# Layer 1's feed-forward as block products, modulation rows dealt out anew, and the chain on block-diagonal 128x128 weights

## The chip, the cores and the metric

One core of a Trainium2 chip runs the whole program. The metric is device microseconds for one execution, the median of the runs; each kernel is also profiled once. The engines are named PE (matrix products; its weight loads are shown apart as PEld), DVE (vector), ACT (scalar functions), POOL (GpSimd) and SP (issues the DMA transfers). Each engine works through its own queue in order and waits for others through semaphores.

## The reference

A two-layer transformer step over 128 prompt tokens and 512 sample tokens, which the kernel treats as T = 640 columns, in two halves of HF = 320. All values are fp32. For each layer:

```python
mod = silu(cond) @ w_mod[l] + b_mod[l]              # 6 x 1024 values for each of 2 conditions
sh_a, sc_a, g_a, sh_f, sc_f, g_f = split(mod, 6)
xn = rmsnorm(h, norm_mix) * (1 + sc_a) + sh_a
proj = xn @ w_in[l]
# three branches (attention, gated linear attention, gated delta net), gates, output projection
h = h + g_a * y
xf = rmsnorm(h, norm_ffn) * (1 + sc_f) + sh_f
gu = xf @ ffn_w_in[l]                               # 1024 -> 2 x 2816
h = h + g_f * ((silu(gu[..., :D_FF]) * gu[..., D_FF:]) @ ffn_w_out[l])
```

The delta net walks over chunks of 64 tokens, 8 heads, in both directions:

```python
v_new = u_n - w_n @ s
o_n   = qd_n @ s + a_n @ v_new
s     = ge_n * s + ke_n.T @ v_new
```

## The kernel before

**The weight stream.** Most of PE's work is one long list of jobs, held by the object `G` (class `Stream`): every 128-column tile of every weight matrix, in a fixed order. A unit of a job takes 4 blocks of 128 rows. Its weights come by DMA into `wr`, are split on ACT (`wh`, the rounded high part, line 514) and on POOL or DVE (`wl`, the rest, lines 518 and 516), and each block makes three products, high x high, high x low, low x high, each on 320 columns, into the PSUM tile `gm`. So one output tile on 8 blocks is 48 matmuls 128x320. When a job ends, its `post` is called (evacuation). `G.to(name)` runs the stream to the end of a job; `fill(name)` slips in as much of the stream as the table `FILL` says at this place. `ahead()` issues the loads for some two units ahead and the split of the next one. Instructions are placed into each engine's queue by a planner which takes the earliest in program order that its model holds ready; an instruction wrapped in `o(...)` while `strict[0]` is set, or given to `keep_in_program_order`, keeps its place.

**Feed-forward.** Output tiles fg (gate) and fu (up) come in 22 pairs. A plain pair is 96 matmuls. The second layer (l = 1 in the code) makes only the first 3 pairs plain (`NPL`), the other 19 as block products: the 2x2 blocks (gate/up x first/second half of the rows) times (row halves x token halves) with 7 block products (`PRODS`) in place of 8, each of 12 matmuls (line 555), so 84 a pair. DVE makes the four sums of weight blocks (`ws`), the low halves `wl` of all seven, and the sums of results (class `Blocks`); ACT takes snapshots of PSUM (`snap`). These are in program order. The 22 tiles are in groups (`GROUPS`): after each group the output products fo (8 of them, over the group's 7, 8 or 11 blocks) are added to h (`h_update`, line 756). The first layer (l = 0) makes all 22 pairs plain, in two groups of 11.

**Modulation.** 16 of the 48 rows of the first layer's `mod` are made on PE at the start. The others, and all of the second layer's, are made on DVE by `ModVe.steps`: a row of weights (`wmt`) by DMA, then two products with sum (line 638), one for each condition. With `nh` = 2 a row comes in two halves of 512 (two tiles, four products), with `nh` = 1 in one of 1024 (two products). Before: rows 16 to 35 of the first layer in its chain (`nh` = 2, one product at each site, the rest after the loop), 36 to 39 in wo, 40 to 47 and all 48 of the second layer in the posts of fu of the first layer's feed-forward (`nh` = 1, kept in program order). The buffers for `wmt` are 4.

**The chain.** `gdn_chain` walks over the delta net's chunks for one pair of heads p; four pairs a layer, on the two directions at once, with 10 steps. A step has up to three products for each direction: with k (result `cy`, line 1066), with t (results `vs` on DVE, line 1078, and `VN` on ACT, line 1081), with kt (new state `S`, line 1092), with `fill` between them and a modulation site (`msite` 3) after the last. `mm_heads` makes each product as two matmuls, one for each head, on 64x64 weights that lie on the partitions of the head (line 1041). After the loop come the products with q (line 1115, block-diagonal 128x128 already) and a, the norm, and five transposes. `chain_load` brings t0, t1, k, kt, q, a of the next pair.

## Time and profile before

| | us |
|---|---|
| median of 3 runs | 2867.09 (2866.7 to 2870.57) |
| profiled execution | 2866.79 |
| its span (first to last instruction) | 2865.0 |
| PE busy | 2681.8 (94%) |
| DVE, ACT, POOL busy | 1699.1, 1290.1, 1075.7 |
| first layer: chain, then wo, then feed-forward | about 644 to 893, to 972, to 1457 |
| second layer: chain, then merge and wo, then feed-forward | about 2075 to 2314, to 2394, to 2853 |

The stages are read off the timeline by the lines that only they use. A row of the timeline merges neighbouring instructions of one kind: start, length, engine, line, operation, tiles (out<-in), shapes (weights rows\*columns, then moving), count, and in brackets the idle time before it with what ended it. The length of a matmul holds its run through the pipeline, so the pace is read from the starts.

### The profile page before, as it was taken

To read this page: it belongs to the slowest core of one execution; us is meant where nothing else is said; L and a number is where in the kernel's file an instruction comes from. 1 tells how busy PE (TensorE), PEld (TensorE's weight loads), DVE (VectorE), ACT (ScalarE), POOL (GpSimd) and SP (SyncE) were. 2 spreads that over 40 slices of the span, in tenths; PEclk is the share of its full clock that TensorE was granted. 3 is DMA by queue.
4 is the path that set the end of the run, shared out by engine and by line. 5 is a ranking of instruction groups with operands and counts; after the bars stand their busy time and mean duration, and the time that the engine had idled before them with its cause. 6 is when DMAs were issued, how large, how long until landed. Compare 5 with 4: busy or idle time off the path is not lost. (4 is left out here: it accounts for less than half of the span.)

```text
span 2865.0 us, 49715 instructions
## 1 busy us (share of the span) xinstructions
PE 2681.8 (94%) x19216; PEld 2461.6 (86%) x19216; DVE 1699.1 (59%) x3141; ACT 1290.1 (45%) x2431; POOL 1075.7 (38%) x777
## 2 busy tenths in 40 slices
PE   6889999899999999999998899997999998999998
PEld 4788887787878899999988888886877898999997
DVE  4765684647655699268456666757434345637373
ACT  5665655543333522122356646565333336425254
POOL 3543222343425467456544432333433254120203
PEclk9999999999999999999999999998999999999999
DMA  6254433245542355335323444232433331222222
GB/s 207 90 163 142 94 77 100 81 113 175 151 113 86 133 175 181 107 123 159 114 80 106 152 136 95 73 97 76 118 98 84 84 108 52 85 85 78 78 80 79
DMA packets 291836, 317.10 MB, mean 111 GB/s; under 512 B 163696, under 2 KB 174768, under 8 KB 291472
## 3 DMA queue, kind: packets, MB, share of 16 engines
q1 hardware_dynamic: 291600, 313.92, 37.4%
q8 instruction: 152, 2.49, 0.4%
q14 instruction: 84, 0.69, 0.1%
HBM read 266.01 MB, written 47.82 MB: 110 GB/s over the span
## 5 line engine op out<-in xcount | busy, mean ns | idle before, releaser
L518 POOL TENSOR_TENSOR wl<-wr,wh 128x512 fp32r<-128x512 f32 (+1 forms) x500 | 723.3, 1450 | 1407.0 <-ACT wh L514 1287.0
L563 PE MATMUL gm<-xh,wh 128*128 128x320 f32 x2848 | 706.2, 324 | 25.6 <-ACT xh L713 7.0
L563 PE MATMUL gm<-xl,wh 128*128 128x320 f32 x2848 | 692.0, 318 | 10.1 <-DVE xl L720 4.2
L563 PE MATMUL gm<-xh,wl 128*128 128x320 f32 x2848 | 687.3, 317 | 15.0 <-POOL wl L518 15.0
L514 ACT ACTIVATE wh<-wr 128x512 fp32r<-128x512 f32 (+1 forms) x538 | 332.4, 621 | 703.7 <-PE gm L563 441.6
L563 PEld LDWEIGHTS gm<-xh,wh 128*128 128x128 f32 x2848 | 487.3, 193 | 50.9 <-ACT xh L713 9.9
L563 PEld LDWEIGHTS gm<-xl,wh 128*128 128x128 f32 x2848 | 491.8, 192 | 27.0 <-DVE xl L720 9.0
L563 PEld LDWEIGHTS gm<-xh,wl 128*128 128x128 f32 x2848 | 489.5, 192 | 23.9 <-POOL wl L518 17.5
L638 DVE CUSTOM_DVE_ANT_0 ctb<-wmt,cbb 128x1024 f32<-128x1024 f32 (+1 forms) x200 | 298.2, 1491 | 3.4
L756 DVE SCALAR_TENSOR_TENSOR h<-gm,mod,h 128x128 f32<-128x128 f32 x168 | 63.8, 433 | 248.7 <-PE gm L563 248.6
L563 PE MATMUL gm<-ah,wh 128*128 128x320 f32 x704 | 164.2, 310 | 0.4 <-DVE h L756 0.2
L563 PE MATMUL gm<-ah,wl 128*128 128x320 f32 x704 | 163.3, 309 | 0.5 <-POOL wl L518 0.5
L563 PE MATMUL gm<-al,wh 128*128 128x320 f32 x704 | 163.3, 309 | 0.0
L1081 ACT ACTIVATE VN<-ch 64x64 f32<-64x64 f32 x320 | 69.9, 219 | 179.7 <-DVE vs L1078 165.5
L563 PEld LDWEIGHTS gm<-ah,wh 128*128 128x128 f32 x704 | 118.3, 188 | 1.7 <-DVE h L756 1.4
L563 PEld LDWEIGHTS gm<-ah,wl 128*128 128x128 f32 x704 | 118.4, 188 | 0.8 <-POOL wl L518 0.8
L563 PEld LDWEIGHTS gm<-al,wh 128*128 128x128 f32 x704 | 118.5, 188 | 0.2
L563 PE MATMUL gm<-ol,wh 128*128 128x320 f32 x384 | 99.0, 331 | 1.5 <-POOL ol L568 1.5
L563 PE MATMUL gm<-oh,wh 128*128 128x320 f32 x384 | 98.4, 333 | 0.5 <-DVE gth L1756 0.3
L563 PE MATMUL gm<-oh,wl 128*128 128x320 f32 x384 | 96.1, 326 | 0.0
L555 PE MATMUL gm<-xh,wl 128*128 128x320 f32 x304 | 94.0, 309 | 0.0
L555 PE MATMUL gm<-xl,wh 128*128 128x320 f32 x304 | 93.9, 309 | 0.0
(793 smaller groups left out, 4743.8 us busy)
## 6 DMA issues: line engine op xcount, KB each, us to landing
wr<-in_wall_dram SPq DMA_DIRECT2D x394, 256.0 KB, 3.0
wmt<-in_wmodt_dram SPq DMA_DIRECT2D x60, 512.0 KB, 3.7
wr<-in_wfo_dram SPq DMA_DIRECT2D x64, 256.0 KB, 2.7
wr<-in_wbr_dram SPq DMA_DIRECT2D x48, 256.0 KB, 2.7
wmt<-in_wmodt_dram SPq DMA_DIRECT2D x40, 256.0 KB, 3.4
wq<-in_wall_dram SPq DMA_DIRECT2D x38, 256.0 KB, 3.1
wm<-in_wmod_dram SPq DMA_DIRECT2D x16, 512.0 KB, 8.4
wr<-in_wfo_dram SPq DMA_DIRECT2D x32, 192.0 KB, 2.4
```

Of the source, the lines that this page charges most:

```text
L514: o(se.activation(wh[:, :w], wr[:, :w], AF.Copy))
L518: ge.tensor_tensor(wl[:, :w], wr[:, :w], wh[:, :w], op=ALU.subtract)
L555: o(pe.matmul(ps, w_[:, wsl], x_[k], start=(start and i == 0), stop=(stop and i == 2), skip_group_check=True))
L563: o(pe.matmul(ps[:, c, :HF], w_[:, wsl], x_[kx][:, c * HF:(c + 1) * HF], start=(start and i == 0), stop=(stop and i == 2)))
L638: ins = ve.tensor_tensor_reduce(self.t, wm, self.c[:, i], 0.5, 0.0, ALU.mult, ALU.add, accum_out=acc[h][:, m - m0, i:i + 1])
L756: o(ve.scalar_tensor_tensor(hs[d][:, s:e], ps[:, c, s - c * HF:e - c * HF], g[:, d, i:i + 1], hs[d][:, s:e], op0=ALU.mult, op1=ALU.add))
L1081: se.activation(VN[d * 64:(d + 1) * 64, h, n], ps[h * 64:(h + 1) * 64, 1], AF.Copy)
```

## The change

The first layer's feed-forward takes the second's form (3 plain pairs, 19 as block products, groups of 8, 7, 7). Its fu posts no longer make all modulation: rows 40 to 47 are begun in wo and ended in the posts of fu1 and fu2; of the second layer's 48 rows the first 24 are made behind the posts of fo (five products, four, four), rows 24 to 39 in the second layer's chain, 40 to 47 in its wo. All use `nh` = 2 with two buffers. Each modulation site of the chain makes two products. t0, t1, k and kt lie block-diagonally in 128x128, with zeros set once by memsets; `mm_heads` becomes one matmul. The tiles o, t and o2 of the chain move to the shared ring `th`, and the ring of snapshots has three slots in place of four. The gate function of the first layer's feed-forward becomes Silu, as in the second, and the factor 0.5 of its row group 5 goes.

```diff
-GROUPS = (((0, 11), (11, 22)), ((0, 8), (8, 15), (15, 22)))
-NPL = (22, 3)
+GROUPS = ((0, 8), (8, 15), (15, 22))
+NPL = 3
...
-                        if OPT["pin"] in (1, 2 + self.nh):
+                        if strict[0] or OPT["pin"] in (1, 2 + self.nh):
...
-        elif s == 2 or s == 5 and mod is mods[0]:
+        elif s == 2:
...
-            if n in ("k", "kt"):
-                dma(B[n], SPL[n][p])
-                continue
...
-                elif n == "q":
+                elif n in ("q", "k", "kt"):
                     dma(B[n][hh, :, hh], SPL[n][p, hh])
                 else:
-                    dma(B[n][hh], TB[int(n[1])][p, h].rearrange("n s c -> s n c"))
-
-    def mm_heads(out, w, x):
-        for h in range(2):
-            hh = slice(h * 64, (h + 1) * 64)
-            pe.matmul(out[hh], w[hh], x[hh], start=True, stop=True)
+                    dma(B[n][hh, :, hh], TB[int(n[1])][p, h].rearrange("n s c -> s n c"))
...
-                    mm_heads(ps[:, 0], B["k"][:, n], S[:, n, d])
+                    pe.matmul(ps[:, 0], B["k"][:, n], S[:, n, d], start=True, stop=True)
...
-                mm_heads(ps[:, 1], B[f"t{d}"][:, n], y)
+                pe.matmul(ps[:, 1], B[f"t{d}"][:, n], y, start=True, stop=True)
...
-                    mm_heads(ps[:, 2], B["kt"][:, n], vs)
+                    pe.matmul(ps[:, 2], B["kt"][:, n], vs, start=True, stop=True)
...
-        o = kp.tile([P, NCH, 64], F32, name="co", tag="co")
-        t = kp.tile([P, 2, 5, 64], F32, name="ct", tag="ct")
+        o = vn(tmp())
+        t = tmp().rearrange("p (d j v) -> p d j v", d=2, j=5)
...
-        o2 = kp.tile([P, NCH, 64], F32, name="co2", tag="ct")
+        o2 = vn(tmp())
...
-            t = self.s[q.name, i] = self.sn.tile([P, HF], F32, name="sn", tag="sn", bufs=4)
+            t = self.s[q.name, i] = self.sn.tile([P, HF], F32, name="sn", tag="sn", bufs=3)
...
-                    for n in ("t0", "t1", "k", "kt"):
-                        bufs[n] = bd.tile([P, NCH, 64], F32, name="bd_" + n)
-                    bufs["q"] = bd.tile([P, NCH, P], F32, name="bd_q")
-                    mst = ModVe(bd, 4, 2).steps(0, range(16, 16 + OPT["mc"])) if l == 0 else iter(())
-                    for h in range(2):
-                        ge.memset(bufs["q"][h * 64:(h + 1) * 64, :, (1 - h) * 64:(2 - h) * 64], 0.0)
+                    for n in ("t0", "t1", "kt", "k", "q"):
+                        bufs[n] = bd.tile([P, NCH, P], F32, name="bd_" + n)
+                    mst = ModVe(bd, 2, 2).steps(l, range(16, 16 + OPT["mc"]) if l == 0 else range(24, 40))
+                    for n in ("t0", "t1", "kt", "k", "q"):
+                        for h in range(2):
+                            ge.memset(bufs[n][h * 64:(h + 1) * 64, :, (1 - h) * 64:(2 - h) * 64], 0.0)
                     chain_load(0, bufs, ("t0", "t1", "k", "kt"))
                     chain_load(0, bufs, ("q", "a"))
...
-                        gdn_chain(l, p, SC, bufs, kp, z[p], fill, lambda: next(mst, None))
+                        gdn_chain(l, p, SC, bufs, kp, z[p], fill, lambda: (next(mst, None), next(mst, None)))
...
-                    if l == 0:
-                        mod_fix(mod, prm, 2)
+                    for s_ in (2,) if l == 0 else (3, 4):
+                        mod_fix(mod, prm, s_)
...
-        mv = ModVe(mvp, 4, 1) if l + 1 < L else None
+        mv = ModVe(mvp, 2, 2)
+
+        def some(gen, n):
+            for _ in range(n):
+                if next(gen, 0) == 0:
+                    break
+
+        mv0 = mv.steps(l, range(16 + OPT["mc"], 40)) if l == 0 else iter(())
+        mv1 = mv.steps(l, range(40, 48))
+        nxt = mv.steps(l + 1, range(24)) if l + 1 < L else iter(())
         nm = Norm()
         resid_posts([f"wo{d}.{l}" for d in range(8)], hs, mod[:, 16:24], nm)
         for d in range(7):
             G.to(f"wo{d}.{l}")
-            if l == 0:
-                mv.run(0, range(16 + OPT["mc"] + (24 - OPT["mc"]) * min(d, 5) // 5, 16 + OPT["mc"] + (24 - OPT["mc"]) * min(d + 1, 5) // 5))
+            if l == 0 and d < 4:
+                some(mv0, 4)
+            else:
+                some(mv1, 5)
+        some(mv0, 1000)
         if l == 0:
             mod_fix(mod, prm, 3)
             mod_fix(mod, prm, 4)
+        else:
+            some(mv1, 1000)
+            mod_fix(mod, prm, 5)
...
-                    if l == 0:
-                        se.activation(v3(th), ps, AF.Tanh, scale=0.5)
-                        ve.scalar_tensor_tensor(v3(th), v3(th), 1.0, ps, op0=ALU.add, op1=ALU.mult)
-                    else:
-                        se.activation(v3(th), ps, AF.Silu)
+                    se.activation(v3(th), ps, AF.Silu)
...
-                    if l + 1 < L:
-                        if l == 0 and f < 8:
-                            mv.run(0, [40 + f])
-                            if f == 7:
-                                mod_fix(mod, prm, 5)
-                        mv.run(l + 1, range(48 * f // NF, 48 * (f + 1) // NF))
+                    if l == 0 and f:
+                        some(mv1, 8 if f < npl - 1 else 1000)
+                        if f == npl - 1:
+                            mod_fix(mod, prm, 5)
...
+            def fo_post(gi, d):
+                def post(ps):
+                    h_update(hs, d, ps, mod[:, 40:48])
+                    some(nxt, 4 if gi else 5)
+                return post
...
-                        G.posts[f"fo{gi}_{d}.{l}"] = lambda ps, d=d: h_update(hs, d, ps, mod[:, 40:48])
+                        G.posts[f"fo{gi}_{d}.{l}"] = fo_post(gi, d)
             nm = Norm()
             resid_posts([f"fo{gl_}_{d}.{l}" for d in range(8)], hs, mod[:, 40:48], nm, l + 1 < L)
+            for d in range(6):
+                n = f"fo{gl_}_{d}.{l}"
+
+                def after(*args, post=G.posts[n]):
+                    post(*args)
+                    some(nxt, 4)
+                G.posts[n] = after
...
-                for s_ in range(6):
+                some(nxt, 1000)
+                for s_ in range(3):
                     mod_fix(mods[l + 1], prms[l + 1], s_)
```

## Rows read from the trace of the kernel before

**Rows 1.** Windows: busy us (instructions) of PE, PEld, DVE, ACT, POOL; granted clock; DMA share, GB/s.

```profile
644.00:893.00 249.00, 243.03 (x2061) 196.28 (x2060) 156.98 (x475) 85.78 (x237) 79.16 (x64) 0.98 0.45 130
2075.00:2314.00 239.00, 233.79 (x2036) 189.93 (x2036) 93.44 (x307) 82.67 (x232) 73.08 (x63) 0.99 0.32 86
972.00:1457.00 485.00, 477.84 (x3198) 472.67 (x3197) 316.09 (x392) 128.74 (x217) 273.19 (x167) 0.99 0.43 133
2394.00:2853.00 459.00, 448.17 (x2981) 441.29 (x2979) 259.54 (x465) 210.57 (x366) 89.41 (x68) 0.99 0.24 73
```

**Rows 2.** Window of 55 us inside the second layer's block products.

```profile
2465.00:2520.00 55.00, 55.00 (x377) 55.00 (x376) 42.05 (x73) 29.75 (x54) 0.00 (x0) 1.00 0.26 82
```

**Rows 3.** Timeline of PE around two bursts of the chain.

```profile
666.20 0.31 PE L563 MATMUL gm<-xh,wh 128*128 128x320 f32 x1
666.44 0.33 PE L1041 MATMUL ch<-vs,bd_kt 64*64 64x64 f32 x4
666.71 0.41 PE L563 MATMUL gm<-xh,wh 128*128 128x320 f32 x1
666.95 0.45 PE L563 MATMUL gm<-xl,wh 128*128 128x320 f32 x2
...
2292.00 0.45 PE L563 MATMUL gm<-xh,wl 128*128 128x320 f32 x2
2292.39 0.45 PE L1041 MATMUL ch<-S,bd_k 64*64 64x64 f32 x8
2292.77 0.56 PE L563 MATMUL gm<-xh,wh 128*128 128x320 f32 x2
2293.16 0.45 PE L563 MATMUL gm<-xl,wh 128*128 128x320 f32 x2
```

**Rows 4.** Timeline of PE: the first and the last of 332 bursts.

```profile
645.51 0.45 PE L1041 MATMUL ch<-cvt,bd_t 64*64 64x64 f32 x8 [0.82 <-DMA cvt<-spl_vt]
...
2298.91 0.28 PE L1041 MATMUL ch<-cy__23305,bd_t 64*64 64x64 f32 x4
```

**Rows 5.** Timeline of PE: small products on 128*128 weights.

```profile
44.58 0.95 PE L608 MATMUL pmt<-C_base,mr 128*128 128x2 f32 x8
...
1577.72 1.05 PE L923 MATMUL pk<-kq,kbd 128*128 128x128 f32 x8
1578.53 0.54 PE L563 MATMUL gm<-xh,wh 128*128 128x320 f32 x2
1578.90 0.45 PE L563 MATMUL gm<-xl,wh 128*128 128x320 f32 x2
```

**Rows 6.** Timeline: one step of the second layer's chain.

```profile
2150.41 0.45 PE L1041 MATMUL ch<-S,bd_k 64*64 64x64 f32 x8
...
2152.14 0.92 ACT L1081 ACTIVATE VN<-ch 64x64 f32<-64x64 f32 x4
...
2153.35 0.33 PE L1041 MATMUL ch<-vs,bd_kt 64*64 64x64 f32 x4
...
2154.39 0.39 PE L1041 MATMUL ch<-S,bd_k 64*64 64x64 f32 x6
```

**Rows 7.** Groups of instructions by line and shape: busy us, mean ns.

```profile
L638 DVE CUSTOM_DVE_ANT_0 ctb<-wmt,cbb 128x512 f32<-128x512 f32 x80 | 68.7, 859 | 0.3
```

**Rows 8.** Timeline: from fo to blocks, second layer.

```profile
2580.34 1.13 DVE L756 SCALAR_TENSOR_TENSOR h<-gm,mod,h 128x128 f32<-128x128 f32 x3 [5.31 <-PE gm L563]
...
2581.39 1.28 DVE L516 TENSOR_TENSOR wl<-ws,wh 128x512 fp32r<-128x512 f32 x2
...
2582.19 0.35 PE L555 MATMUL gm<-xh,wl 128*128 128x320 f32 x1
```

**Rows 9.** Timeline of DVE: one product that runs alone.

```profile
690.76 0.68 DVE L638 CUSTOM_DVE_ANT_0 ctb<-wmt,cbb 128x512 f32<-128x512 f32 x1
```

**Rows 10.** DMA issues by line: count, KB each, median us to landing.

```profile
wmt<-in_wmodt_dram SPq DMA_DIRECT2D x40, 256.0 KB, 3.4
```

**Rows 11.** Waits of the SP queue, first layer's feed-forward: total us, times, longest.

```profile
SPq L429 <- DVE mod L638: 162.7, 50, 4.5
```

More of the change, by code (lines that the diff above doesn't have):

```diff
@@ L1678, in tile_hybrid @@
             k8(f"wo{d}", "post" if d == 7 else None)
-        gr, npl = GROUPS[l], NPL[l]
+        gr, npl = GROUPS, NPL
         pairs = {f: Pair(f"ff{f}.{l}", a["wall"][l, TILES[f"fg{f}"]], a["wall"][l, TILES[f"fu{f}"]]) for f in range(npl, NF)}
@@ L1981, in tile_hybrid @@
             mod_fix(mod, prm, 4)
+        else:
+            some(mv1, 1000)
+            mod_fix(mod, prm, 5)
         mark(f"normf{l}")
-        gr, npl = GROUPS[l], NPL[l]
+        gr, npl = GROUPS, NPL
         if npl < NF:
```

## The prediction

> **What bounds the kernel now.** I read the stretches by stage first [rows 1]: in both chain stages and both feed-forwards PE is busy 97 to 99% of the time, at a granted clock of 0.98 to 0.99 (the upper level, 2.4 GHz); apart from PE's own weight loads nothing passes 66%. So time is saved by giving PE less to do, unless something else becomes late where PE was the cover. "Busy" hides one thing, though, and the reader should look at starts rather than durations. In an undisturbed stretch PE starts 377 matmuls in 55.00 us, 0.146 us each [rows 2]; I use 0.147. Against that grid the timeline around the chain's small matmuls shows holes [rows 3].
>
> **The chain: what a burst costs.** From the start of the pair of gm matmuls at 2292.00 to the start of that at 2293.16 pass 1.16 us; the two pairs take 0.59 of it, so the burst of 8 passes on 64\*64 weights costs 0.57 [rows 3]. From 666.20 to 666.95 pass 0.75 us with two gm matmuls (0.29): a burst of 4 costs 0.46. Four more passes add 0.11 to 0.12, about 0.03 each; the rest, 0.34, is a constant for each burst, before it and after it. Counting uninterrupted bursts over both layers gives 332 [rows 4]. The passes are 56 calls a pair (18 with k, 20 with t, 18 with kt) x 2 heads x 2 passes (a call on fp32 shows as 2 instructions a head) x 8 pairs = 1792. Price now: 332 x 0.34 + 1792 x 0.03 = 113 + 54 = 167 us.
>
> After, each call is one matmul on 128\*128 weights: 896 passes of 64 columns. No row has that shape, so it is bounded by 128 columns and by 2. Eight passes on 128\*128 with 128 columns start at 1577.72, with no idle time noted before them; then follow a pair of gm at 1578.53 and the next pair at 1578.90. Less the first pair's 0.29, 1.18 leaves 0.89 for eight, 0.111 each. With 2 columns, eight passes last 0.95 against 1.05 [rows 5]: a difference of 0.10 over all eight, no more than the last one's own length, so the pace hardly depends on the columns and 64 of them should cost the same 0.111. New price 896 x 0.111 = 100 us, without a constant. PE's relief is 167 - 100 = 67 us.
>
> The Trainium skill, TensorE: Matmul & The Clock Gate, Part 3 (packing small matmuls by row and column tiling), speaks against this: tiles on different row groups run side by side, so two small matmuls cost hardly more than one. By that rule alone a pair of heads is already cheap, the block-diagonal form is a loss of 100 - 54 = 46 us, and the sum below would end at +37 us. The rows agree on the 0.03 us a pass and disagree on the 0.34 around each burst, which the rule leaves out.
>
> **How much of the relief arrives.** The chain is also a sequence of waits, and with shorter bursts these come to the front. A step of the second layer [rows 6]: k at 2150.41, VN (four copies, 0.92 us) from 2152.14, so until 2153.06, the second kt at 2153.35, the next k at 2154.39: 3.98 us. Without gm in between, the second kt can follow VN's end at once (0.28 earlier). The next k starts 1.04 after kt; a 0.28 us update of S and some 0.5 us of passing on between the engines are needed, so about 0.2 can go. Together 0.45 to 0.5 off, a floor near 3.5 us. In 80 steps that is 36 us: the lower bound, if the waits set the pace everywhere; 67 is the upper, if PE does. The stretches between the pairs of heads are full of gm and give what PE gives. I take 50.
>
> Against it stand the modulation rows. The second layer's chain gets 16 of them: 64 products of 128x512, 0.86 us each [rows 7], 55 us of DVE in a stage where DVE is busy 93 of 239 [rows 1]. If all were exposed, 55; if all fell into DVE's pauses, nothing. The nearest row is the first layer's chain, which has 80 of them already: 249 us against 239, and of these 10 us 25 more PE instructions (2061 against 2036) explain 4. So 6 for 80 products, 5 for 64; I take 6, as the floor leaves less room. The first layer keeps its 80, now two at a site.
>
> Small things: eight more memsets a layer on POOL ahead of the first loads, and k and kt loaded in two transfers each of 256 B pieces instead of one. The same loads already exist for t and q; they lie under the gm of the stretch between pairs. 0 to 5 us a layer, I take 1 in all. **Chain: -50 + 6 + 1 = -43.**
>
> **The feed-forward of the first layer.** 19 of its 22 pairs go from 96 to 84 matmuls: 228 x 0.147 = 33.4 us less. The second layer already runs in this form; its stage is 459 us against 485, 26 less with 217 fewer instructions (31.9) [rows 1], so some 6 go at the edges (token sums, start). I take -28.
>
> What DVE does in the blocks costs nothing there: 42 of 55 us busy with PE without a gap [rows 2]. But the modulation of the next layer now sits behind the outputs fo0, fo1, fo2: five, four and four products after each, in program order while the blocks run. Inside a fo phase that fits: one output is 8 x 6 x 0.147 = 7.0 us of PE in the first group and 6.2 in the others; DVE needs 1.1 for the update [rows 8] and 4.3 or 3.4 for the products at 0.86 [rows 7]. At the change from fo to blocks it doesn't. In the second layer now the last update runs 2580.34 to 2581.47, the two low halves behind it 2581.39 to 2582.67, and the first of these is wanted by the third matmul of the second block product at 2582.19 [rows 8]: about 0.1 us to spare. POOL is idle there, so I price the products at the 0.68 of one that runs alone [rows 9], not at the mean: five put ahead cost 3.4 us, four 2.7. So two stalls of 3.3 and 2.6, 6 together. Two buffers for the rows add to this: a row's half lands 3.4 us after its issue [rows 10], so two halves can't be turned over faster than about every 5.5 us, against 2.5 halves wanted in 7.0 in the first group; lag 0 to 3 us, taken as 1. The remaining rows of the gate (40 to 47), now put behind fu1 and fu2 just ahead of the blocks, 0 to 5, taken as 2. The SP queue waits 162.7 us for DVE to free such buffers in this stage today, at most 4.5 at once, and PE doesn't notice [rows 11]; its cover is the weight loads issued two units (7 us) ahead. **Feed-forward: -28 + 6 + 1 + 2 = -19.**
>
> **The output projection** wo (7.0 us an output): five products an output in the second layer, 4.3 + 1.1 and the sum of squares, just about PE's pace; in the first four, then five. A lag at the end of each delays the norm directly: 0 to 4 each, taken as 3 in all.
>
> **Sum.** -43 - 19 + 3 = -59. Profiled execution 2866.79 (span 2865.0), 0.3 under the median 2867.09: 2866.8 - 59 = 2808.
>
> **The rivals.**
> *DVE paces the chain.* The doubled site puts two products (1.7 us) between the update of S and the next step; if they are scheduled there rather than into pauses, each site adds about 1.2 us to a 3.5 us floor, and 36 sites a layer eat the 43 us. For it: DVE rises to some 148 of 239 us; against it: the first layer's chain bears 80 now for 6 us. Then -19 + 3 = -16: 2851.
> *The feed-forward gives all back.* DVE in program order and an SP queue in which a weight load stands behind a row waiting for one of two buffers: about 3 us at each output with a third half (8 in the first group, 3 and 6 in wo) is some 50 us at worst, 25 if half are exposed, against a gain of 19. For it: buffers halved; against: the 162.7 us of SP waits that cost nothing. Then -43 + 3 = -40: 2827.
> *Slower: the small tiles were the cheap form.* If the 0.34 us around a burst belongs to the waits for DVE and ACT, and not to the small tiles, it stays, and only the passes change: +46. Then 46 + 6 + 1 - 19 + 3 = +37: 2904. The sign turns where less than 37 / 332 = 0.11 us of the constant goes. The page of the Trainium skill named above would have it so. Against it: the same gap stands at bursts with very different things in front of them, and the full-array burst has none [rows 3, 5].
> *No change* would be a mixture of the first two.
>
> **Chances.** Forecast 0.63, feed-forward given back 0.14, DVE paces the chain 0.12, no change 0.04, slower 0.07. Under 0.2% (5.7 us) a measurement of this kernel can't tell a change from none; so faster 0.63 + 0.14 + 0.12 = 0.89, same 0.04, slower 0.07. The forecast's own range is from -95 (chain -67, feed-forward -28) to -36. The whole range reaches up to the chain rival, 2852, and down to 2772; outside lie the slower case, no change and part of the chain rival.
>
> **What would show it.** Right: bursts on 128\*128 with gm on either side at 0.111 a pass and no hole; about 228 fewer gm matmuls in a first feed-forward near 466 us; chain stages of about 225 and 220 us; PE pauses of 3 to 4 us only at the two changes from fo to blocks. Wrong: a hole that stays around the bursts, PE waiting for DVE products or cy in the chain, PE waiting for wl or wr in fo or wo, or a granted clock that falls where pauses open.

## The result, and the profile after

The changed kernel takes 2895.2 us (median of 4 runs, 2888.0 to 2897.02), the kernel before 2868.6 beside it: ratio 1.0088, 95% interval 1.0068 to 1.0108. It is 27 us slower; 59 us faster was forecast. The profiled execution took 2896.81 us, its span is 2895.0 (30.0 more) and its mean granted clock 0.951 (before 0.968).

The windows of the changed kernel by stage (columns as in [rows 1]; first chain, first feed-forward, second chain, second feed-forward):

```profile
644.00:890.00 246.00, 230.83 (x1655) 217.78 (x1653) 159.92 (x477) 85.82 (x239) 82.04 (x67) 0.95 0.49 136
985.00:1475.00 490.00, 457.65 (x2964) 448.87 (x2962) 359.18 (x703) 216.90 (x386) 103.29 (x75) 0.95 0.35 109
2085.00:2329.00 244.00, 229.00 (x1638) 216.42 (x1637) 147.52 (x438) 85.46 (x237) 77.22 (x64) 0.95 0.46 126
2430.00:2880.00 450.00, 440.42 (x2946) 435.83 (x2947) 257.39 (x461) 205.23 (x358) 87.90 (x67) 0.98 0.24 74
```

The reader should look at PE and the clock together. PE has less to do, as planned: 2964 instructions in the first feed-forward against 3198 in [rows 1], some 400 fewer in each chain. But where it was busy 97 to 99% of the time at 0.98 to 0.99 it is now busy 93 to 94% at 0.95: pauses have opened, and the clock has fallen with them. Only the last stage, which the change left alone, kept its numbers.

I cut both traces at the same points, the first PE matmul of each stretch of products, and every later kernel too (us; "chain" runs from the last undisturbed product stretch ahead of it to wo's first matmul, "wo" to the feed-forward's first, "ffn" of the first layer to the first of the next layer, "between" from there to the second chain; median and ratio of the kernel in the last columns):

| kernel | chain 1 | wo 1 | ffn 1 | between | chain 2 | wo 2 | ffn 2 | median | ratio (95%) |
|---|---|---|---|---|---|---|---|---|---|
| before | 287.0 | 64.2 | 479.6 | 599.2 | 280.6 | 62.8 | 441.8 | 2868.6 | 1 |
| after | 279.2 | 78.9 | 484.3 | 597.6 | 283.2 | 78.1 | 441.4 | 2895.2 | 1.0088 (1.0068, 1.0108) |
| e1_chain | 279.6 | 62.9 | 479.9 | 605.3 | 269.8 | 62.8 | 441.8 | 2854.7 | 0.9958 (0.9945, 0.9970) |
| e2_ffn | 303.7 | 77.8 | 480.7 | 602.6 | 295.1 | 79.0 | 441.5 | 2935.3 | 1.0245 (1.0227, 1.0264) |
| e3_norows | 279.7 | 62.8 | 453.6 | 600.5 | 285.5 | 62.8 | 441.9 | 2842.8 | 0.9916 (0.9895, 0.9936) |
| e4_noch2 | 278.2 | 78.2 | 484.6 | 601.6 | 269.9 | 80.2 | 441.5 | 2879.0 | 1.0046 (1.0031, 1.0061) |
| e5_cond | 282.0 | 75.1 | 473.4 | 598.9 | 279.8 | 78.2 | 441.4 | 2879.2 | 1.0040 (1.0027, 1.0054) |
| e6_nonxt | 279.7 | 78.7 | 458.0 | 603.9 | 283.1 | 78.1 | 441.5 | 2873.6 | 1.0015 (0.9997, 1.0032) |
| e7_split | 311.0 | 62.9 | 479.6 | 598.9 | 291.3 | 62.8 | 441.8 | 2899.0 | 1.0106 (1.0087, 1.0125) |
| e8_double | 297.8 | 63.6 | 479.6 | 599.6 | 277.4 | 62.8 | 443.2 | 2887.7 | 1.0065 (1.0038, 1.0092) |
| e9_vnlate | 286.0 | 62.9 | 479.3 | 606.2 | 270.1 | 62.8 | 441.8 | 2857.6 | 0.9964 (0.9951, 0.9977) |
| e10_vnsb | 279.2 | 63.0 | 479.3 | 602.7 | 266.1 | 62.8 | 441.8 | 2845.6 | 0.9922 (0.9907, 0.9937) |
| e11_moved | 296.0 | 75.6 | 464.7 | 604.5 | 299.0 | 62.8 | 444.5 | 2899.4 | 1.0115 (1.0097, 1.0134) |
| e12_pinned | 279.4 | 78.1 | 480.1 | 603.5 | 285.5 | 76.2 | 441.5 | 2893.8 | 1.0095 (1.0078, 1.0112) |
| e13_tiles_vnsb | 286.4 | 62.8 | 479.3 | 598.6 | 278.2 | 62.8 | 441.8 | 2870.4 | 1.0029 (0.9997, 1.0061) |
| e14_best | 284.8 | 69.4 | 464.0 | 605.1 | 273.3 | 68.3 | 441.5 | 2854.6 | 0.9959 (0.9949, 0.9970) |
| e15_memset | 276.3 | 63.5 | 480.4 | 607.5 | 263.6 | 62.8 | 441.8 | 2846.7 | 0.9926 (0.9911, 0.9940) |
| e16_best2 | 284.6 | 69.1 | 470.0 | 603.6 | 271.0 | 68.6 | 441.4 | 2851.6 | 0.9945 (0.9929, 0.9960) |

From before to after: chains -7.8 and +2.6, wo +14.7 and +15.3, first feed-forward +4.7, all else about 0. "Between" holds no changed line and still ranges from 597.6 to 607.5, so a total is good to some 5 us, and what a part costs is read from its own stage. A stage length comes from the one profiled execution, which lies 6 to 12 us above its kernel's median in e4, e14 and e16 and 9 to 11 below it in e13 and e8. The largest single part of this lies in matmuls near its end (windows on the same stretch, before and in e15, columns as above):

```profile
2018.89:2045.84 26.95, 24.12 (x198) 21.03 (x197) 16.40 (x30) 11.83 (x22) 9.91 (x6) 1.00 0.20 62
2013.06:2043.47 30.41, 27.10 (x198) 23.33 (x197) 16.44 (x31) 12.55 (x23) 9.91 (x6) 0.89 0.19 61
```

The same 198 PE instructions take 3.5 us more at a granted clock of 0.89 than at 1.00; e1, e6, e9 and e10 show the 0.89 there too, the changed kernel and e13 the 1.00.

**The passes are what they were priced at.** The timeline of PE around a burst on 128\*128 weights in the changed kernel:

```profile
2131.43 0.46 PE L563 MATMUL gm<-oh,wl 128*128 128x320 f32 x2
2131.72 0.55 PE L1051 MATMUL ch<-S,bd_k 128*128 128x64 f32 x4
2132.08 0.54 PE L563 MATMUL gm<-xh,wh 128*128 128x320 f32 x2
2132.46 0.31 PE L563 MATMUL gm<-xl,wh 128*128 128x320 f32 x1
```

From the gm pair at 2131.43 to the single gm matmul at 2132.46 pass 1.03 us; four gm matmuls take 0.59 of them, so four passes cost 0.44, 0.11 each, with 64 columns and no hole beside them. That is the price worked out from [rows 5]; the hole of [rows 3] is gone from an undisturbed burst.

**Few bursts are undisturbed, though.** One line's instructions, the kt products of the changed kernel: duration, and what ended the idle time in front of them, matmuls and weight loads taken together. The last row is the same for all chain products of the kernel before:

```profile
L1079 PE MATMUL ch<-vs,bd_kt x288: 217/275/475, 650.0 to 2314.4; 128*128 128x64 f32 x144
...
its engine sat idle before it (us, times) until:
  ACT VN L1073: 34.6, 81
  DVE vs L1070: 0.3, 1
...
  ACT VN L1081: 12.0, 41
```

81 idle times in front of kt end with the copies of VN; before there were 41, with a third of the time. The matmuls alone waited 10.5 us for VN in the changed kernel (21 times), before 2.3 us (5 times).

**wo.** PE's waits in the second wo of the changed kernel (total us, times, longest), then a piece of its timeline:

```profile
PE cs L696 <- DVE nacc L687: 5.0, 1, 5.0
PE gm L563 <- ACT wh L514: 2.9, 3, 1.7
PE gm L563 <- POOL wl L518: 2.9, 4, 1.0
```

```profile
2409.97 0.69 DVE L638 CUSTOM_DVE_ANT_0 ctb<-wmt,cbb 128x512 f32<-128x512 f32 x1
...
2410.58 1.13 DVE L756 SCALAR_TENSOR_TENSOR h<-gm,mod,h 128x128 f32<-128x128 f32 x3
...
2411.75 0.74 ACT L686 ACTIVATE th<-h 128x640 f32<-128x640 f32 x1 [0.38 <-DVE h L756]
2412.39 0.71 ACT L702 ACTIVATE us<-h,mod 128x512 f32<-128x512 f32 x1
2413.00 1.14 ACT L514 ACTIVATE wh<-wr 128x512 fp32r<-128x512 f32 x2
2413.67 0.41 PE L563 MATMUL gm<-xh,wh 128*128 128x320 f32 x1 [1.73 <-ACT wh L514]
2413.69 3.20 POOL L518 TENSOR_TENSOR wl<-wr,wh 128x512 fp32r<-128x512 f32 x2 [5.06 <-ACT wh L514]
2413.98 1.75 DVE L638 CUSTOM_DVE_ANT_0 ctb<-wmt,cbb 128x512 f32<-128x512 f32 x1
2415.24 0.41 PE L563 MATMUL gm<-xh,wl 128*128 128x320 f32 x1 [1.02 <-POOL wl L518]
```

This is one chain of delays: the product ends, h is updated, th and us follow on ACT, and the weight half wh stands behind them; PE waits 1.73, then 1.02 more for POOL's low half. At the end the sum of squares (nacc) is 5.0 late, and that goes into the norm undiminished. The second wo as a whole, before and after:

```profile
2341.00:2404.00 63.00, 59.61 (x395) 57.66 (x393) 19.30 (x36) 28.80 (x49) 27.84 (x22) 1.00 0.39 130
2356.00:2434.00 78.00, 63.83 (x394) 59.88 (x392) 54.79 (x106) 30.49 (x54) 31.92 (x23) 0.96 0.53 172
```

Of the 15 us, PE's idle time makes 10.8; for the other 4.2 it is busy longer with the same work, at a clock of 0.96 in place of 1.00. DVE, at 54.8 of 78, is not full: what delays PE is when its results come.

**From fo to the blocks.** Timeline of the changed kernel at the first of the two changes, then windows on it (columns as above):

```profile
1174.35 0.69 DVE L638 CUSTOM_DVE_ANT_0 ctb<-wmt,cbb 128x512 f32<-128x512 f32 x1 [1.38 <-DMA wmt<-in_wmodt_dram]
...
1176.05 1.14 DVE L756 SCALAR_TENSOR_TENSOR h<-gm,mod,h 128x128 f32<-128x128 f32 x3 [0.39 <-PE gm L563]
...
1180.52 0.69 DVE L638 CUSTOM_DVE_ANT_0 ctb<-wmt,cbb 128x512 f32<-128x512 f32 x1 [1.26 <-DMA wmt<-in_wmodt_dram]
...
1181.87 1.29 DVE L516 TENSOR_TENSOR wl<-ws,wh 128x512 fp32r<-128x512 f32 x2
1182.61 0.63 PE L555 MATMUL gm<-xh,wl 128*128 128x320 f32 x1 [4.55 <-DVE wl L516]
```

```profile
1165.00:1177.00 12.00, 12.00 (x84) 12.00 (x83) 8.20 (x25) 2.53 (x4) 1.29 (x1) 1.00 0.48 152
1177.00:1182.60 5.60, 1.06 (x8) 0.80 (x6) 4.24 (x13) 0.96 (x2) 0.00 (x0) 0.92 0.29 95
1182.60:1187.00 4.40, 4.39 (x16) 4.39 (x17) 2.69 (x5) 0.63 (x1) 0.00 (x0) 0.50 0.17 60
1187.00:1192.00 5.00, 5.00 (x31) 5.00 (x31) 1.93 (x4) 1.92 (x4) 0.00 (x0) 0.85 0.15 52
```

In the kernel before the low halves followed the last update at once [rows 8]; now the products stand between them, as predicted, with the wait for a row's load (two buffers) on top: 4.55 us where 3.3 were priced. New to me are the windows. After the stall PE is busy without a break, and the granted clock is 0.50 (1.2 GHz, the lower level) for the next 4.4 us: 16 matmuls instead of 30. The pause costs its length and about half as much again (the 14 missing matmuls alone are 2.1 us).

### The profile page after: what moved, and what is told of

Same layout as the page of the kernel before. It is cut to its first block, busy times and chain, and to the rows that moved or that the text cites. A ratio compares the mean times of both kernels' runs of the same rounds, so it can differ in the third digit from the quotient of the medians.

```text
span 2895.0 us, 48260 instructions
## 1 busy us (share of the span) xinstructions
PE 2647.5 (91%) x18092; PEld 2483.2 (86%) x18092; DVE 1858.4 (64%) x3711; ACT 1378.2 (48%) x2605; POOL 914.8 (32%) x698
## 5 line engine op out<-in xcount | busy, mean ns | idle before, releaser
L518 POOL TENSOR_TENSOR wl<-wr,wh 128x512 fp32r<-128x512 f32 (+1 forms) x424 | 600.1, 1420 | 1575.1 <-ACT wh L514 1462.5
L514 ACT ACTIVATE wh<-wr 128x512 fp32r<-128x512 f32 x500 | 306.0, 619 | 420.8 <-PE gm L563 227.7
L563 PEld LDWEIGHTS gm<-xh,wh 128*128 128x128 f32 x2240 | 393.4, 197 | 51.0 <-ACT wh L514 11.4
L563 PEld LDWEIGHTS gm<-xh,wl 128*128 128x128 f32 x2240 | 393.3, 196 | 29.9 <-POOL wl L518 27.9
L563 PEld LDWEIGHTS gm<-xl,wh 128*128 128x128 f32 x2240 | 394.9, 196 | 24.6 <-DVE xl L734 8.8
L638 DVE CUSTOM_DVE_ANT_0 ctb<-wmt,cbb 128x512 f32<-128x512 f32 x320 | 286.9, 896 | 31.6 <-DMA wmt<-in_wmodt_dram 27.3
L514 ACT ACTIVATE wh<-ws 128x512 fp32r<-128x512 f32 x152 | 95.6, 630 | 128.3 <-PE gm L555 72.9
L1073 ACT ACTIVATE VN<-ch 64x64 f32<-64x64 f32 x320 | 69.6, 217 | 178.8 <-DVE vs L1070 160.9
L555 PE MATMUL gm<-xeh,wh 128*128 128x320 f32 x456 | 141.5, 310 | 1.5 <-ACT sn L1580 1.5
L555 PE MATMUL gm<-xeh,wl 128*128 128x320 f32 x456 | 141.5, 310 | 0.9 <-DVE wl L516 0.9
L555 PE MATMUL gm<-xel,wh 128*128 128x320 f32 x456 | 141.8, 311 | 0.0
```

The source lines that it names most:

```text
L514: o(se.activation(wh[:, :w], wr[:, :w], AF.Copy))
L518: ge.tensor_tensor(wl[:, :w], wr[:, :w], wh[:, :w], op=ALU.subtract)
L555: o(pe.matmul(ps, w_[:, wsl], x_[k], start=(start and i == 0), stop=(stop and i == 2), skip_group_check=True))
L563: o(pe.matmul(ps[:, c, :HF], w_[:, wsl], x_[kx][:, c * HF:(c + 1) * HF], start=(start and i == 0), stop=(stop and i == 2)))
L638: ins = ve.tensor_tensor_reduce(self.t, wm, self.c[:, i], 0.5, 0.0, ALU.mult, ALU.add, accum_out=acc[h][:, m - m0, i:i + 1])
L1073: se.activation(VN[d * 64:(d + 1) * 64, h, n], ps[h * 64:(h + 1) * 64, 1], AF.Copy)
```

## The experiments

Theory A at the outset: the rows dealt out anew ate the gain, the chain form is sound but waits leave little of its relief. Rival B: the small tiles were the cheap form. Rival C: block products gain nothing in the first layer.

**e1_chain: the chain part alone.** The kernel before with lines such as these, and two row buffers in the first chain:

```
-                    mm_heads(ps[:, 0], B["k"][:, n], S[:, n, d])
+                    pe.matmul(ps[:, 0], B["k"][:, n], S[:, n, d], start=True, stop=True)
```

> The kernel before with the chain on block-diagonal weights and nothing else (two row buffers in place of four in the first chain, since the wider weights take the space). Prediction as it stands: -50 + 1, so about 2820. Theory A (the rows that were dealt out anew ate the gain, the chain form itself is sound but its waits leave little of the relief): -10 to -20, 2849 to 2859. Rival B (the small tiles were the cheap form, the passes cost more and the constant stays): +10 to +46, 2879 to 2915.

2854.7, -12: the form gains (B falls), but not the 49 forecast. By stages -7.4 and -10.8, together -18 ("between" came out 6 longer). From the first to the last chain matmul I added up what PE spends beside the 0.147 of each gm matmul wherever a chain matmul begins or ends an interval: 83.5 and 74.3 us a layer before, 69.6 and 59.8 here. That is 28 us less. The passes alone are 448 x 0.111 = 49.7 a layer, so 30 us are left beside them in both layers, where the price of 100 had assumed none; about 16 of these are noted as idle time of PE there (before, 6). The stages keep 18 of the 28: from their start to the first chain matmul they are 2.6 and 4.2 us longer (e15 returns to that).

**e2_ffn: the feed-forward part alone.** The changed kernel with the chain of the kernel before (64\*64 weights, four buffers).

> The changed kernel with the chain back on 64x64 weights, so block products and rows dealt out anew alone (the 64 products of the second chain included). Prediction as it stands: -19 + 3 + 6 = -10, about 2859. Theory A: wo and norm +30, feed-forward +5, second chain +5, so about 2909. Rival C (the block products in the first layer gain nothing, rows or not): the same time; the run without rows has to tell C from A.

2935.3, +68, worse than either expectation. wo and ffn are as in the changed kernel; the excess is in the chains, 303.7 and 295.1. So the same rows cost the chains more on the small tiles; e8 looks at that.

**e3_norows: no rows outside the chains.**

> The changed kernel without the modulation rows in wo, norm and the first feed-forward (256 row products less 144 in the chains stay out; the modulation there is a constant). Theory A: both wo stretches back to 53 to 54 us and their gaps to 10, the first feed-forward at 455 to 460: -30 and -25 to -30, about 2837. Rivals B and C: at most -10, 2885 or more.

2842.8, -52. Both wo are at 62.8 (before 64.2 and 62.8), and the first feed-forward falls to 453.6: the block products gain 26.0 against the kernel before (C falls), and the rows cost 484.3 - 453.6 = 30.7 there and 16.1 + 15.3 in wo. PE's waits in the second wo are back to these three:

```profile
PE cs L698 <- ACT th L693: 1.9, 1, 1.9
PE gm L563 <- DVE h L758: 0.2, 1, 0.2
PE cs L698 <- ACT nacc L575: 0.2, 1, 0.2
```

**e4_noch2: no products in the second chain.**

> The changed kernel without the 64 products in the second layer's chain (those scale and shift rows are a constant). Prediction as it stands: -5. If DVE's products pace the chain (the rival of the prediction): -20 or more. If neither, because DVE's pauses hold them: 0.

Chain 2 goes from 283.2 to 269.9: 64 products cost 13.3 us, 0.21 each, twice my 6; the median says 16. The form's own gain there is 280.6 - 269.9 = 10.7, the same as in e1.

**e5_cond: the condition vectors kept.** After the first use they are written to DRAM; later users only load them.

```
+            if h in kept:
+                dma(self.c, CKEEP[h])
+                return
```

> The changed kernel, in which the prepared condition vectors (the tanh of line 624 and its product) are made once in the first chain, kept in DRAM and only loaded again by each later user. If the 15 us a layer in wo come from tanh standing in front of the weight halves on ACT and from DVE's part of that preparation: wo back to about 55, gap to 12, so -20, about 2875. If they come from the row products on DVE and from waiting for the load of the vectors: 0 to -5, 2890 to 2895.

2879.2, -16: ffn 1 -10.9, wo 1 -3.8, chain 2 -3.4, against +2.8 in chain 1, where the vectors are now written too. wo 2 stays at 78.2. So tanh ahead of the weight halves has a part in the first layer, and in the second wo it makes no difference: there DVE waits for the loads of the rows instead. In the changed kernel it had waited 4.3 us for them and 7.6 for tanh; here:

```profile
DVE ctb L646 <- DMA wmt<-in_wmodt_dram: 12.8, 5, 5.6
```

**e6_nonxt: no rows behind fo0, fo1, fo2.**

> The changed kernel without the 24 rows of the next layer's modulation behind the outputs fo0, fo1 and fo2 (those 96 products stay out, that modulation is a constant). The run without any rows moved the first feed-forward from 471 to 442 us. If the rows behind the outputs did that, by stalls at the change to the blocks and the lower clock after each: -20 to -25, 2870 to 2875, with the first group (x and block 0, in front of fo0) still long by 8 to 10. The prediction had 6 + 1 for these rows: 2888.

2873.6, -22; ffn 1 458.0, -26.3, and PE keeps 0.147 us a matmul through both changes to the blocks. I had priced these rows at 6 + 1. The remaining 4.4 to e3 are the rows behind fu1 and fu2 (priced 2).

Cut at its jobs, the first feed-forward shows where the 30.7 lie (changed kernel less e3): 5.5 in the three plain pairs, 3.1 in the first blocks, 0 in fo0, 7.3 in the blocks behind it, 3.6 in fo1, 4.2 in the blocks behind that, 6.9 in the last fo with the norm. e6 keeps only 4.8 in the plain pairs; e5 takes out the 3.1 and the 3.6. So the two changes from fo to blocks make 11.5, and the last fo, where the norm waits as behind wo, 6.9.

**e8_double: two products at a site, kernel before.**

```
-  lambda: next(mst, None)
+  lambda: (next(mst, None), next(mst, None))
```

> The kernel before with two modulation products at each site of the first chain in place of one, and nothing else. The run with the rows and block products but 64x64 weights had this stage 16 us longer than before, the changed kernel with the same two products at each site did not. If two products at a site delay the chain on 64x64 weights (DVE paces it there): +16, about 2883. If the site does not matter: 2867.

2887.7, +21, with six runs from 2874.6 to 2896.2; the profiled one took 2876.3, and in it chain 1 is +10.8 on the small tiles, so the price may be higher. On block-diagonal weights two a site (after, 279.2) and one (e1, 279.6) are alike; the buffers differ too (four here, two there), so whether the form or the buffers tell is not separated. By these stages, two thirds of e2's excess in chain 1 is this.

**e7_split, e9_vnlate, e10_vnsb: what holds the chain back.** All three start from e1. e7 gives kt a PSUM tile of its own, for which the two directions must share tiles; e9 puts the copies of VN behind kt in the program; e10 reads PSUM once:

```
+  vb = kp.tile([P, 64], F32, name="vb", tag="vb", bufs=2)
+  se.activation(vb, ps[:, 1], AF.Copy)
   for h in range(2):
-      se.activation(VN[d * 64:(d + 1) * 64, h, n], ps[h * 64:(h + 1) * 64, 1], AF.Copy)
+      se.activation(VN[d * 64:(d + 1) * 64, h, n], vb[h * 64:(h + 1) * 64], AF.Copy)
```

> The kernel of the run with the chain alone (2854.7), with the result of kt in a PSUM tile of its own, so that kt no longer stands behind the four copies of VN on ACT. If this wait is what holds back the relief of PE: 0.3 to 0.5 us in each of 72 steps, so -20 to -35, 2820 to 2835. If the chain is held by its sequence through DVE anyway (the two directions now share one tile): 0 to -5, 2850 to 2855.

> The kernel of the run with the chain alone (2854.7), with the four copies of VN put behind the kt matmuls in the order of the program, each direction keeping its own PSUM tile. If kt's wait for VN paces the chain: some 0.4 us in each of 72 steps, -15 to -30, 2825 to 2840. If the copies only move to the next wait (the next k then waits for the tile that VN reads): 0, about 2855.

> The kernel of the run with the chain alone, with VN read from PSUM by one copy of 128x64 on ACT into SBUF, from which the two copies of 64x64 are made behind it. kt then waits for one ACT operation a direction in place of two. If the wait for VN paces the chain: about 0.2 us a direction where both directions are bound, 72 steps, -10 to -20, 2835 to 2845. If not: 0, or a little more for the added ACT work (144 x 0.2 us), 2855 to 2860.

e7 missed in the instructive direction: +44 against e1, chains 311.0 and 291.3. PE's wait for vs in front of kt in its first chain, then the same in e1, then DVE's waits in e7:

```profile
PE ch L1081 <- DVE vs L1071: 11.2, 25, 2.2
...
PE ch L1079 <- DVE vs L1070: 0.3, 1, 0.3
```

```profile
DVE vs L1071 <- PE ch L1065: 33.3, 25, 8.8
...
DVE vs L1071 <- ACT VN L1074: 8.2, 14, 1.2
```

VN is off kt's path, but vs now waits for VN, for which it has no wait in e1's first chain: the two share a tile. Here the added waits between engines inside the step cost more than all of PE's relief. e9 moved the wait on and gained nothing (chain 1 +6.4, chain 2 +0.3), as its second expectation said, though the next k waits for S (6.5 us in chain 1, 2.2 in e1) and for VN only once, 0.8 us. e10 gained: 2845.6. The idle time in front of kt that ACT ended, matmuls and weight loads together, falls from 26.2 us (57 times) in e1 to

```profile
  ACT vb L1073: 21.2, 54
```

in e10 (of the matmuls alone from 8.6 to 7.3 us), the excess to 66.8 and 55.1, chain 2 by 3.7. Of the 9 us between the medians the stages show 4; the rest lies in stretches without a changed line.

**e13_tiles_vnsb: the same VN on the small tiles.**

> The kernel before, on its 64x64 weights, with VN read from PSUM by one copy a direction and parted in SBUF, as in the run that gained 9 us on the block-diagonal weights (2845.6). If the wait for VN is common to both forms and the block-diagonal one saves PE time of its own: -5 to -9 here, 2858 to 2862, so that the form is still worth 12 to 17. If the form itself gains nothing once the wait is shorter (packed small tiles are as cheap): about 2846. If PE paces the chain on 64x64 weights: 0, 2867.

2870.4, 3 over the kernel before and not the 2858 to 2862 of the first expectation. The ten runs reach from 2859.4 to 2902.6, and the profiled one, 2861.9, is one of the quickest. In it the chains take 286.4 and 278.2: 3.0 less than before, and 19.3 more than e10. So by the stages of single executions the form is worth 18 us with the old VN and 19 with the new; by the medians it is 12 and 25.

**e11_moved and e12_pinned: other places, and a fixed order.** e11 puts three products at a site (96 in each chain), none in wo 2, six behind each of the first six outputs of fo0 and fo1, and keeps the vectors as e5 does. e12 is the changed kernel with the products outside the chains kept in program order.

> The changed kernel with the same rows in other places: 24 rows in the first chain and 24 in the second (three products a site), 4 products behind each of the first four outputs of the first wo and none in the second, six behind each of the first six outputs of fo0 and fo1 and none behind the last two, and the prepared condition vectors kept in DRAM. If the place of the rows is what the change lost by: both wo back to 53 to 57 with gaps of 10 to 12 (-25), PE without a stall at the changes to the blocks (-15), chains +10: 2850 to 2865. If the rows cost as much wherever they lie: 2880 to 2895.

> The changed kernel with the row products of wo and the first feed-forward bound to their place in the program on DVE (as the kernel before had them with its 1024-wide products; in the changed kernel those of wo are free, and the trace shows all 32 of each wo pulled in between its outputs and ahead of their updates of h). If the pulled-forward products delay the updates, behind them us and the weight halves on ACT, and so PE: wo back to 54 to 57 and the gap to about 12 in the second layer (-8 to -10 a layer), 2875 to 2883. If the number of products in wo is what counts and not their order: 2890 to 2897.

e11 failed as a whole and was right in its parts: wo 2 back at 62.8, the blocks after fo0 at PE's own pace, ffn 1 -19.6. But the chains rise to 296.0 and 299.0: 16 more products cost 17 in the first, 32 more cost 16 in the second. That fits the rival "DVE paces the chain", setting in at the third product of a site: e14 has the same 96 in its first chain at two a site and takes 284.8 (with VN through SBUF, which gained 0.4 there in e10). Little was gained in wo 1, since the 16 products put behind fu1 and fu2 were scheduled ahead into wo, which held 32 again. e12 answers the question of order: 2893.8, no change; wo 2 76.2. So it is not their order. With no product wo 2 takes 62.8 (e3, e11), with 18 68.3 (e14), with 32 78.1. But each row brings a load as well, and e5 has DVE waiting for these; no run gave the changed wo more than two buffers (the kernel before, with four, made four rows 1024 wide in its first wo and took 64.2 there), so what the products cost by themselves is not separated from what their loads cost. PE's waits in e12's wo 2:

```profile
PE cs L697 <- DVE nacc L688: 6.7, 1, 6.7
PE gm L563 <- ACT wh L514: 2.5, 2, 1.6
...
PE gm L563 <- POOL wl L518: 1.4, 2, 0.9
```

**e14_best, e15_memset, e16_best2.** e14 puts together what had helped: block products, VN through SBUF, vectors kept, 96 and 64 products in the chains at two a site, 18 in each wo, none behind the last two outputs of each fo.

> The changed kernel with all that the runs point to: VN through SBUF, the condition vectors kept in DRAM, 24 rows in the first chain and 16 in the second at two products a site, the products outside the chains bound to their place, three behind each of the first six outputs of both wo and the rest of those 8 rows behind fu0 to fu2, seven or five behind each of the first six outputs of fo0 to fo2 and none behind the last two. If the places are what the change lost by: 2895 - 9 (VN) - 16 (vectors) - 15 to -25 (wo) - 10 to -15 (fo) + 3, so 2835 to 2855. If rows cost some 0.7 us each wherever they go (the chains alone took 0.16 to 0.27 a product): 2860 to 2870.

2854.6, within its first expectation: 41 us better than the change, level with e1. Against e3 the two wo cost 6.6 and 5.5 more, ffn 1 10.4 more.

PE's waits at the start of e1's second chain had shown one of 3.9 us for a low weight half; the timeline of POOL and PE in front of it holds the last of the added memsets (bd_k), and behind them those of q, which the kernel before has too:

```profile
2061.58 1.54 POOL L1934 MEMSET bd_k<- 64x640 f32 x2
...
2067.17 0.86 POOL L1934 MEMSET bd_q<- 64x640 f32 x1
2068.11 1.53 POOL L568 TENSOR_TENSOR ol<-z,oh 128x640 fp32r<-128x640 f32 x1
2069.60 1.26 POOL L518 TENSOR_TENSOR wl<-wr,wh 128x512 fp32r<-128x512 f32 x1
...
2070.91 0.55 PE L563 MATMUL gm<-oh,wl 128*128 128x320 f32 x2 [3.90 <-POOL wl L518]
...
2072.05 0.74 PE L563 MATMUL gm<-oh,wl 128*128 128x320 f32 x2
2072.58 0.74 PE L563 MATMUL gm<-oh,wh 128*128 128x320 f32 x2
```

The two pairs at the end start 0.53 apart in place of 0.29. e15 (from e10) and e16 (from e14) do the added memsets on DVE: `(ge if n == "q" else ve).memset(...)`.

> The kernel of the run with the chain alone and VN through SBUF (2845.6), with the eight added memsets of each layer on DVE in place of POOL. On POOL they take 0.8 us each in front of a low weight half, for which PE then waits 3.9 us at the chain's start, and its pace is 0.27 a matmul in the stretch behind it. If that is what the start of the chain lost (2.7 and 4.3 us): -5 to -9, 2837 to 2841. If DVE is late there in its place, or the loads in two pieces are what is late: 0, 2845.

> The kernel of the run that put all together (2854.6: block products, rows in better places, VN through SBUF), with the same eight memsets on DVE. If the memsets cost the same here: -5 to -9, 2846 to 2850, so that the chain part alone stays the faster one and the block products of the first layer, with the rows that they displace, cost about 9 us in the best arrangement tried.

In e15 that wait is gone, and the chains fall to 276.3 and 263.6, 5.4 less than e10; the median stays (2846.7), since "between" came out 4.8 longer. Of that, 3.0 lie in 96 matmuls near its end, which e15 makes at a granted clock of 0.78 and e10 at 0.85; why the clock differs there is open. e16 is 2851.6, its interval overlapping e14's and e15's. e10 and e15, the chain part with a shorter VN and without the feed-forward part, beat both kernels, the one before by 0.7 to 0.8%.

## Why the prediction was wrong

Step by step, in us of stage lengths:

| step of the prediction | forecast | measured | from |
|---|---|---|---|
| chain: relief and small things | -50 + 1 | -18.2 | e1, both chains |
| 64 products in the second chain | +6 | +13.3 | after less e4 |
| first feed-forward: fewer matmuls | -28 | -26.0 | e3 less before |
| rows in the first feed-forward | +6 + 1 + 2 | +30.7 | after less e3 |
| wo, both layers | +3 | +30.0 | after less before |
| sum | -59 | +29.8 | span: +30.0 |

The sign failed in the two terms for displaced rows: priced at 9 and 3, measured at 31 and 30. Both had been priced as a lag of one engine. For wo I compared DVE's time for an output (4.3 + 1.1 and the sum of squares) with PE's 7.0, found "just about PE's pace", and took 3. The first failure is the time for an output: 4.3 went by 0.86 a product, the mean of the first chain [rows 7]; in the second wo, where POOL makes a low half for every unit, the 32 average 1.01, and one in the timeline above takes 1.75. DVE's waits there for tanh (7.6) and for the rows (4.3) had no term. The second failure is what hangs on a late DVE: h, then th and us on ACT, and behind these the weight halves, in order. "Name what is queued behind" would have been the question; I asked it of the blocks and not of wo. e3 (all of it back when the rows go) and e12 (order without effect) show that it is the rows, wherever in wo they stand; products and loads are not told apart.

In the feed-forward the mechanism was right at the two changes: stalls of 4.5 and 2.6 us stand there, where 3.3 and 2.6 were forecast, and with the slower stretch after each they cost 11.5 of the 30.7. The lower clock after a pause, the preparation of the condition vectors (e5: 10.9 us) and the delay of the norm by the rows in the last fo (6.9) were in no term; the wait for two buffers was priced at 1.

In the chain the price of a pass (0.111) was right, and [rows 3]'s hole did go; I took 50 of 67, and 18 came. The 167 were 158, and of the 67 only 28 left the time around the chain's matmuls (e1). The floor of 3.5 us a step, built from one step [rows 6], was none: from kt to kt the shortest steps take 3.3 us before and 2.9 in e1, while the mean falls only from 4.9 to 4.5 and from 4.7 to 3.9. With PE out of the way, the waits for VN, cy and S come to the front. About 5 us of stage length were the memsets on POOL, priced at 1 (e15). The rule of the Trainium skill that I weighed (TensorE: Matmul & The Clock Gate, Part 3) is borne out for the pass (0.03 against 0.11 us), and the constant that it leaves out was mostly the small tiles' own: of 104 us around the bursts (158 less 1792 x 0.03) 30 remained. The rival that ended slower came near the time, 2904, by the wrong mechanism; that was luck. The rival in which the feed-forward gives all back had the right place and too small a price: 25 to 50 us of lag were named in it, in wo and fo alike, and given a chance of 0.14. Its cause, weight loads behind rows in the SP queue, was not tested by itself.

What stays open: why the granted clock differs between kernels in the unchanged stretch "between", why two products a site cost 10.8 on the small tiles and nothing on the large ones, and what more buffers for the rows would have given back.

## What to carry to other kernels

Before work is moved, list what covers it now. The 26 us that block products save were paid for by pairs that had hidden 56 rows on DVE behind PE; in the places of the change a row of four products cost 0.8 to 1.9 us (13.3 / 16 in the chain, 26.3 / 24 behind fo, 15.3 / 8 in wo), as third product of a site 2 to 4 (e11), and at that price they outweigh the gain.

An engine's idle share in a stage is no cover if the engine's own late result has the next stage's operands queued behind it; follow that queue one engine further than the move.

Where a chain is made cheaper on the engine that bounds it, list the waits between engines within one step first: here 18 of 67 us arrived, and two directions made to share a tile (e7) cost 53 us of stage length.

## What the runs showed of the hardware

A pause of 4.55 us of PE was followed by 4.4 us at a granted clock of 0.50 (1.2 GHz), after 12 us at 1.00; a pause of 3.9 us in e1 by pairs 0.53 us apart in place of 0.29.

A fp32 pass on 128\*128 weights takes 0.11 us with 64 moving columns, as with 128 [rows 5], and unlike the 64\*64 passes it leaves no hole beside it.

The same 128x512 product took 0.69 us with POOL idle and 1.75 while POOL made a low weight half (2413.98, above). Over the whole changed kernel, 190 of the 320 such products have no POOL instruction beside them, and each took 0.67 to 0.69; the other 130 average 1.20, with 2.07 the longest.

The same 198 PE instructions took 26.95 us at a granted clock of 1.00 (before) and 30.41 at 0.89 (e15), in a stretch that no edit touched.
